# Attention scores and transposed weights of two heads in one two-bank PSUM tile, in a written order, the next unit's scores ahead of the softmax

## The chip, the cores and the metric

The kernel runs on one core of a Trainium2 chip. The time is the device time of one execution in microseconds; lower is better. Runs are compared with runs of the kernel before on the same chip.

## The reference, cut to what matters

One decoder layer on a sequence of 256 positions, all in float32: an input projection feeds three token mixers (a convolution module A, a spatial gating unit B and a sparse attention C), whose outputs are gated, added and projected, and a feed-forward part follows. The change concerns the attention C. It has 16 heads of width 64 in 4 groups and three branches that share the queries: compressed blocks, selected blocks and a window. At 256 positions the window and the selection both hold every earlier position, so these two branches are plain causal attention, each with its own keys and values:

```python
def masked_softmax(s, mask):
    s = jnp.where(mask, s.astype(jnp.float32), NEG)
    m = jnp.max(s, axis=-1, keepdims=True)
    e = jnp.where(mask, jnp.exp(s - m), 0.0)
    return e / jnp.maximum(jnp.sum(e, axis=-1, keepdims=True), 1e-30)
...
        s = jnp.einsum("bqghd,bkgd->bghqk", qb, kw)
        p = masked_softmax(s, wmask)
        o_win = jnp.einsum("bghqk,bkgd->bqghd", p.astype(vw.dtype), vw)
        gb = lax.dynamic_slice_in_dim(gates, start, NSA_Q_BLOCK, axis=1)
        return gb[..., 0:1] * o_cmp + gb[..., 1:2] * o_slc + gb[..., 2:3] * o_win
```

## The kernel before

The weights stream through: a piece of 128x1024 is fetched by SyncE, split by ScalarE (line 118, `whi`) and VectorE (line 119, `wlo`) into a high and a low half, and multiplied on TensorE in three products (lines 167 to 169, or 147 and 154). Four split pieces can stand ready; a piece feeds twelve matmuls of 512 columns in the stage of this case.

This stage is `branch(bi, ...)`, run for B, A and C in turn. For each of four column blocks it computes the merge gate (`pg`, from `hT`) and the output projection (`py`, from `Bt`, `At` or `Ct`). Small work of the mixers is written as generators in the queue `bg`; after each group of projection matmuls, `pump` takes steps from the first generator until their estimated times use up a budget. `until("C")` empties the queue up to the mark C before the third projection reads `Ct`. The order thus traced is a priority: a planner then places instructions on each engine, by its own estimates of when their inputs and buffers are ready, earlier ones first. `issue_after(ins)` forces an order on one engine.

The attention runs in the stages of B and A. `attn(qt, gg)` is traced for two query tiles of 128 positions and two head groups, and does two branches (`br`) in it: eight units (qt, gg, br), here numbered 0 to 7 in that order. A unit has four pairs of heads, j = 0..3, r = 0 and 1. Head r of a pair lies in partitions 64r to 64r+63 of `qf` and `kk`, so its score matmul (line 680) uses half of TensorE's rows; its value matmul (line 712) writes half of the columns, partitions 64r onward of `O`. There are 128 keys (qt = 0) or 256 (qt = 1). A unit's steps are: the scores into `ps`, per head r a tile of its own; VectorE adds the mask, takes the maximum and writes `e` (line 685); ScalarE takes the exponential and the sum (line 691) and scales by gate over sum (line 700); TensorE transposes the weights into `pp`, per r and key block (line 706); ScalarE copies them out (line 707); TensorE multiplies with the values into `O` (line 712). `O` starts with the compressed branch (line 664), takes both branches of a (qt, gg) and goes to `Ct`.

PSUM has eight banks: four for the tiles "acc" of the projections and four of the tag "bg", from which `O`, the score tiles, the weight tiles and the small tiles of the other generators (transposes of the input, layer norm sums, spatial gating, compression, merge) are drawn. The weights `e` and their transposes `pt` lie in SBUF tiles of the tag "s8", of which four exist and the keys and queries hold two. "s16" has three larger ones: `At`, `Bt`, `Ct` at this time, later `mh` and `ml`, the operands of the merge, traced ahead of the third branch.

Of the kernel before, what the change touches and what calls it, by code (L numbers as in the profile page):

```python
# [47 lines left out]
def block(ctx: ExitStack, tc: tile.TileContext, x, fp, cst, rows, sgw, w1, w2, wf_a, wt_bv, wf_bu, wf_c,  # L48
# [5 lines left out]
    P0 = ctx.enter_context(tc.tile_pool(name="p0", bufs=1))  # L54
    PS = ctx.enter_context(tc.tile_pool(name="ps", bufs=4, space=PSUM))

    def row(i0, n):
# [124 lines left out]

    marks = set()
    T1 = {}
# [85 lines left out]
    def enter(k):  # L270

        pt = PS.tile([128, T], F32, tag="bg", name=f"pth{k}")
# [50 lines left out]
    for cb in range(2):  # L323
# [26 lines left out]
        if cb == 0:  # L350
            r0 = norm1(ss, "x", 2)
            V.tensor_scalar(rh, r0, 0.5, None, op0=ALU.mult)
            rbp = PS.tile([128, T], F32, tag="bg", name="rbp")
# [51 lines left out]
    def lna_gen():  # L405
        def total(acc, nm):
            ps = PS.tile([128, T], F32, tag="bg", name="lnp" + nm)
            PE.matmul(ps, lhsT=ones, rhs=acc, start=True, stop=True)
            return ps
# [57 lines left out]
    def sg_gen(gi):  # L467
        ps = PS.tile([128, 2, 128], F32, tag="bg", name=f"psg{gi}")
# [61 lines left out]
    def cmp_gen(kv):  # L530
        bk = bk_box[kv]
        zp = PS.tile([128, 2, 256], F32, tag="bg", name=f"zp{kv}")
        for q in range(4):
# [10 lines left out]
        for a in range(2):  # L544
            S.activation(zs[a], zp[:, a], AF.Copy)
        hp = PS.tile([128, 2, 64], F32, tag="bg", name=f"hp{kv}")
        for h in range(2):
# [10 lines left out]
        if kv == 0:  # L558
            ps = PS.tile([128, 64], F32, tag="bg", name="kcp")
            for h in range(2):  # L560
# [4 lines left out]
        else:  # L565
# [6 lines left out]
            for gg in range(2):  # L572
                ps = PS.tile([128, 128], F32, tag="bg", name=f"vcp{gg}")
                for h in range(2):
# [46 lines left out]
    def cmp_attn(qt):  # L621
        ps = PS.tile([128, 2, 4, 2, 16], F32, tag="bg", name=f"sc{qt}")
        for gg in range(2):
# [25 lines left out]
        yield 1300  # L649
        pp = PS.tile([128, 2, 128], F32, tag="bg", name=f"pcp{qt}")  # L650
        for gg in range(2):
# [6 lines left out]

    def attn(qt, gg):


        O = PS.tile([128, 4, 128], F32, tag="bg", name=f"O{qt}{gg}")
        for j in range(4):
            PE.matmul(O[:, j], lhsT=vbd[:, gg, j], rhs=pct[qt][:, gg], start=(j == 0), stop=False,
                      skip_group_check=True)
        nk = (qt + 1) * 128
        mk = cs[:, K_MK + 256 - nk:K_MK + 256]
        hpb = 512 // nk
        half = [slice(0, 64), slice(64, 128)]
        for br in range(2):  # L670
            nm = f"{qt}{gg}{br}"
            ep = [s8([128, 2, 4, 256], F32, f"ep{nm}{r}") for r in range(2)]
            e = [t[:, 0] for t in ep]
            pt = [t[:, 1].rearrange("p a b -> p (a b)").rearrange("p (k c) -> p k c", k=2) for t in ep]
            m = P1.tile([128, 2, 8], F32, tag="am", bufs=2, name="am" + nm)
            for b in range(4 // hpb):
                ps = [PS.tile([128, hpb, nk], F32, tag="bg", name=f"s{nm}{b}{r}") for r in range(2)]
                for jj in range(hpb):
                    for r in range(2):
                        PE.matmul(ps[r][:, jj], lhsT=qf[half[r], gg * 4 + b * hpb + jj, qt * 128:qt * 128 + 128],  # L680
                                  rhs=kk[half[r], gg, br, 0:nk], start=True, stop=True)
                for jj in range(hpb):
                    j = b * hpb + jj
                    for r in range(2):
                        V.tensor_tensor_reduce(e[r][:, j, 0:nk], ps[r][:, jj], mk, 1.0, -3e38, ALU.add, ALU.max,
                                               m[:, r, j:j + 1])
                        yield nk * 1.05 + 130
            V.tensor_scalar(m[:, :, 0:4], m[:, :, 0:4], -1.0, None, op0=ALU.mult)
            for j in range(4):
                for r in range(2):  # L690
# [7 lines left out]
            for j in range(4):  # L698
                for r in range(2):
                    S.activation(e[r][:, j, 0:nk], e[r][:, j, 0:nk], AF.Copy, scale=m[:, r, 4 + j:5 + j])  # L700
                    yield 30
            for kb in range(qt + 1):
# [12 lines left out]
            yield 200  # L715
        Ct = Ct_box["t"]
        ch = Ct[:, gg * 4:gg * 4 + 4, 0, qt * 128:qt * 128 + 128]
        cl = Ct[:, gg * 4:gg * 4 + 4, 1, qt * 128:qt * 128 + 128]
        S.activation(ch, O, AF.Copy)
        V.tensor_sub(cl, O, ch.bitcast(F32))  # L720
        yield 650

# [14 lines left out]
    mac = s16(P0, [128, 2, D], F32, "mac")  # L737
    mh = ml = None

    def branch(bi, act_of):  # L740

        for cb in range(4):
# [43 lines left out]
    def mix_gen(cb):  # L786

        for k in range(4 * cb, 4 * cb + 4):
            pt = PS.tile([128, T], F32, tag="bg", name=f"pm{k}")
            for t in range(2):  # L790
                PE.transpose(pt[:, t * 128:t * 128 + 128], mac[:, t, k * 128:k * 128 + 128], ident)
            S.activation(mh[:, k], pt, AF.Copy, scale=0.5)
            V.scalar_tensor_tensor(ml[:, k], pt, 0.5, mh[:, k].bitcast(F32), op0=ALU.mult, op1=ALU.subtract)
            yield 500
# [3 lines left out]
    until("A")  # L798
    mh = s16(P1, [128, KT, T], R, "mh")
    ml = s16(P1, [128, KT, T], R, "ml")  # L800
    branch(2, lambda: Ct_box["t"])


# [37 lines left out]
    def enter2(t, k):  # L841

        pt = PS.tile([128, 128], F32, tag="bg", name=f"ptf{t}{k}")
        ts = slice(t * 128, t * 128 + 128)
# [91 lines left out]
    for run in lumps(pu2[2], hs, h2):  # L936
        in_line(run)
    rbp2 = PS.tile([128, T], F32, tag="bg", name="rbp2")
    with tc.issue_after(pe_last[0]):
# [194 lines left out]
```

## Time and profile before

| | us |
|---|---|
| median of 3 runs | 1621.16 |
| lowest and highest | 1620.5 and 1622.27 |
| the profiled execution | 1621.49 |
| its span in the profile | 1619.8 |
| TensorE busy with matmuls in it | 1599.5 (99%) |
| VectorE, ScalarE busy | 1125.6 (69%), 855.8 (53%) |

The span reaches from the first to the last instruction of the profiled execution. Busy times are sums over an engine's instructions without overlaps. In the views below a matmul's duration goes to its modelled end, and matmuls overlap, so what one costs in the line is read from the start of one to the start of the next. The tiles are given as written by the program without numbers: `s` scores, `pp` transposed weights, `O` values, `pg` and `py` projections.

### The profile page before, as it was taken

To read this page: it belongs to the slowest core of one execution; us is meant where nothing else is said; L and a number is where in the kernel's file an instruction comes from. 1 tells how busy PE (TensorE), PEld (TensorE's weight loads), DVE (VectorE), ACT (ScalarE), POOL (GpSimd) and SP (SyncE) were. 2 spreads that over 40 slices of the span, in tenths; PEclk is the share of its full clock that TensorE was granted. 3 is DMA by queue.
4 is the path that set the end of the run, shared out by engine and by line. 5 is a ranking of instruction groups with operands and counts; after the bars stand their busy time and mean duration, and the time that the engine had idled before them with its cause. 6 is when DMAs were issued, how large, how long until landed. Compare 5 with 4: busy or idle time off the path is not lost.

```text
span 1619.8 us, 22288 instructions
## 1 busy us (share of the span) xinstructions
PE 1599.5 (99%) x8293; PEld 1352.5 (84%) x8293; DVE 1125.6 (69%) x1914; ACT 855.8 (53%) x1378; POOL 16.1 (1%) x45
## 2 busy tenths in 40 slices
PE   9999998999999999999999999999999999999997
PEld 6888887888887767788888888888888888888886
DVE  6799999887655554455566877777777777444444
ACT  6554444475466655644455655555555555344342
POOL 0000020000000000000000000000000000000000
PEclk9999999999999999999999999999999999999999
DMA  8655556557644444555772655555555556666663
GB/s 296 226 197 182 186 157 200 184 181 244 204 144 155 159 130 139 186 185 191 239 249 83 195 190 189 187 192 192 185 189 193 190 184 201 212 193 194 192 192 115
DMA packets 85437, 303.74 MB, mean 188 GB/s; under 512 B 9808, under 2 KB 10192, under 8 KB 84688
## 3 DMA queue, kind: packets, MB, share of 16 engines
q1 hardware_dynamic: 84096, 298.04, 56.5%
q0 software_dynamic: 944, 4.19, 0.7%
q8 instruction: 65, 1.06, 0.3%
q14 instruction: 44, 0.36, 0.1%
q10 hardware_dynamic: 288, 0.08, 0.0%
HBM read 299.13 MB, written 2.10 MB: 186 GB/s over the span
## 4 chain that ended last, share of the span: by engine, by line
PE 96%; DVE 2%; DMA 1%; issue 0%; ACT 0%; SPq 0%; DVEq 0%; ACTq 0%
PE ps L147 28%; PE ps L154 15%; PE po L168 7%; PE po L169 7%; PE po L167 7%; PE pg L167 5%; PE pg L168 5%; PE pg L169 5%; PE py L167 3%; PE py L169 3%; PE py L168 3%; PE s L680 1%; PE pv L167 1%; PE O L712 1%; PE pv L168 1%; PE pv L169 1%
## 5 line engine op out<-in xcount | busy, mean ns | idle before, releaser
L119 DVE TENSOR_TENSOR wlo<-wraw,whi 128x1024 fp32r<-128x1024 f32 (+1 forms) x533 | 642.8, 1208 | 294.6 <-ACT whi L118 287.5
L118 ACT ACTIVATE whi<-wraw 128x1024 fp32r<-128x1024 f32 (+1 forms) x533 | 554.9, 1044 | 382.2 <-PE po L169 135.7
L147 PE MATMUL ps<-h2T,whi 128*128 128x512 f32 x1360 | 324.6, 391 | 0.0
L147 PEld LDWEIGHTS ps<-h2T,whi 128*128 128x128 f32 x1360 | 250.0, 188 | 48.3
L154 PEld LDWEIGHTS ps<-h2T,wlo 128*128 128x128 f32 x1360 | 174.4, 191 | 6.6
L154 PE MATMUL ps<-h2T,wlo 128*128 128x256 f32 x1360 | 176.7, 283 | 0.0
L147 PE MATMUL ps<-hT,whi 128*128 128x512 f32 x640 | 158.1, 394 | 3.1 <-ACT gsg L607 3.1
L169 PE MATMUL pg<-whi,hT 128*128 128x512 f32 x384 | 151.0, 393 | 0.0
L168 PE MATMUL pg<-wlo,hT 128*128 128x512 f32 x384 | 151.0, 393 | 0.0
L167 PE MATMUL pg<-whi,hT 128*128 128x512 f32 x384 | 148.9, 394 | 0.0
L190 ACT ACTIVATE t<-ps 128x256 f32<-128x256 f32 x125 | 47.5, 382 | 174.3 <-PE ps L147 174.3
L147 PEld LDWEIGHTS ps<-hT,whi 128*128 128x128 f32 x640 | 117.3, 190 | 25.3 <-ACT gsg L607 3.3
L167 PE MATMUL po<-whi,gh 128*128 128x512 f32 x336 | 130.7, 389 | 0.0
L168 PE MATMUL po<-wlo,gh 128*128 128x512 f32 x336 | 130.7, 389 | 0.0
L169 PE MATMUL po<-whi,gl 128*128 128x512 f32 x336 | 130.7, 389 | 0.0
L191 DVE TENSOR_TENSOR t<-ps,t 128x256 f32<-128x256 f32 x125 | 52.8, 423 | 91.6 <-ACT t L190 91.5
L401 DVE SCALAR_TENSOR_TENSOR cv<-hb,fps,cv 128x256 f32<-128x256 f32 x240 | 105.3, 479 | 0.8 <-ACT cv L397 0.7
L154 PEld LDWEIGHTS ps<-hT,wlo 128*128 128x128 f32 x640 | 84.4, 191 | 4.4
L154 PE MATMUL ps<-hT,wlo 128*128 128x256 f32 x640 | 86.1, 283 | 0.0
L169 PEld LDWEIGHTS pg<-whi,hT 128*128 128x128 f32 x384 | 72.1, 188 | 16.1 <-issue 1.5
L168 PEld LDWEIGHTS pg<-wlo,hT 128*128 128x128 f32 x384 | 72.1, 188 | 16.0 <-issue 1.3
L167 PEld LDWEIGHTS pg<-whi,hT 128*128 128x128 f32 x384 | 71.9, 188 | 15.6 <-issue 1.0
(297 smaller groups left out, 1923.0 us busy)
## 6 DMA issues: line engine op xcount, KB each, us to landing
wraw<-in_wf_up_dram SPq DMA_DIRECT2D x176, 512.0 KB, 4.2
wraw<-in_wt_g_dram SPq DMA_DIRECT2D x96, 512.0 KB, 3.7
wraw<-in_wt_dn_dram SPq DMA_DIRECT2D x88, 512.0 KB, 3.6
wraw<-in_wt_p_dram SPq DMA_DIRECT2D x48, 512.0 KB, 3.7
wraw<-in_wf_a_dram SPq DMA_DIRECT2D x32, 512.0 KB, 3.9
wraw<-in_wt_o_dram SPq DMA_DIRECT2D x32, 512.0 KB, 4.5
wraw<-in_wt_bv_dram SPq DMA_DIRECT2D x16, 512.0 KB, 6.3
wraw<-in_wf_bu_dram SPq DMA_DIRECT2D x16, 512.0 KB, 4.3
```

The costliest lines, as they stand in the source:

```text
L118: S.activation(hi[:, :n], raw[:, :n], AF.Copy)
L119: V.tensor_sub(lo[:, :n], raw[:, :n], hi[:, :n].bitcast(F32))
L147: ins = PE.matmul(ps[:, :, ts], lhsT=ws[k // 8][0][:, c:c + 128], rhs=mov[:, k, :, ts], start=(k == 0 and not t), stop=(k == n - 1), skip_ ...
L154: ins = PE.matmul(ps[:, 1, ts], lhsT=ws[k // 8][1][:, c:c + 128], rhs=mov[:, k, 0, ts], start=False, stop=False, skip_group_check=True).ins
L167: PE.matmul(ps, lhsT=xh, rhs=hi, start=first, stop=False)
L168: PE.matmul(ps, lhsT=xh, rhs=lo, start=False, stop=False)
L169: return PE.matmul(ps, lhsT=xl, rhs=hi, start=False, stop=last).ins
L190: S.activation(t1, ps[:, 1], AF.Copy)
L191: V.tensor_add(t1 if rb is not None else dst, ps[:, 0], t1)
L401: V.scalar_tensor_tensor(ca[:, j], hb[:, j, k:k + T], w(j, k), ca[:, j], op0=ALU.mult, op1=ALU.add)
L680: PE.matmul(ps[r][:, jj], lhsT=qf[half[r], gg * 4 + b * hpb + jj, qt * 128:qt * 128 + 128], rhs=kk[half[r], gg, br, 0:nk], start=True, sto ...
L712: PE.matmul(O[half[r]].rearrange("p j t -> p (j t)"), lhsT=vsw[:, kb, v0:v0 + 64], rhs=pt[r][:, kb], start=False, stop=((br, kb, r) == (1, ...
```

## The change

PSUM: the four single banks move into a pool of their own, which can be closed and reopened. For the attention it holds two single banks (`bank`, used by `O`) and one tile of two banks (`two_banks`); before and behind the attention it holds four singles again. `attn` becomes eight `Unit`s with three generators: `scores`, `weights` and `values`. The scores of both heads go to one two-bank tile, one bank for each r, and so do the transposed weights of a key block. The score matmuls and the value matmuls are chained by `in_turns`, r = 1 and r = 0 alternating, the values from the last key block to the first; the two copies out of a weight tile are chained too. The scores of unit n + 1 are traced before the softmax of unit n. The units of the second branch have `e` and `pt` in a tile `ep` of the tag "s16"; the compressed branch's matmuls come behind the first transposes; `mh` and `ml` are allocated behind `until("C")`. Elsewhere `PS.tile(..., tag="bg")` becomes `bank(...)`.

```diff
+    PB = {}
+    def banks(single, double):
+        if PB:
+            PB["ctx"].close()
+        PB["ctx"] = ctx.enter_context(ExitStack())
+        PB["pool"] = PB["ctx"].enter_context(tc.tile_pool(name=f"pb{single}{len(marks)}", bufs=single, space=PSUM))
+        PB["double"] = double
+    def bank(shape, name):
+        return PB["pool"].tile(shape, F32, tag="bg", name=name)
+    def two_banks(shape, name):
+        return PB["pool"].tile(shape, F32, tag="bg2", bufs=PB["double"], name=name)
...
+    banks(4, 0)
...
+    def in_turns(work):
+        last = None
+        for out, lhsT, rhs, start, stop in work:
+            with ExitStack() as order:
+                if last is not None:
+                    order.enter_context(tc.issue_after(last))
+                last = PE.matmul(out, lhsT=lhsT, rhs=rhs, start=start, stop=stop, skip_group_check=True).ins
...
+            ep = [Ct_box["ep"][:, r] if br else s8([128, 2, 4, 256], F32, f"ep{self.nm}{r}") for r in range(2)]
...
             for b in range(4 // hpb):
-                ps = [PS.tile([128, hpb, nk], F32, tag="bg", name=f"s{nm}{b}{r}") for r in range(2)]
-                for jj in range(hpb):
-                    for r in range(2):
-                        PE.matmul(ps[r][:, jj], lhsT=qf[half[r], gg * 4 + b * hpb + jj, qt * 128:qt * 128 + 128],
-                                  rhs=kk[half[r], gg, br, 0:nk], start=True, stop=True)
+                ps = two_banks([128, 2, hpb, nk], f"s{self.nm}{b}")
+                in_turns([(ps[:, r, jj], qf[half[r], gg * 4 + b * hpb + jj, qt * 128:qt * 128 + 128],
+                           kk[half[r], gg, br, 0:nk], True, True) for jj in range(hpb) for r in (1, 0)])
...
             for kb in range(qt + 1):
-                pp = [PS.tile([128, 4, 128], F32, tag="bg", name=f"pp{nm}{kb}{r}") for r in range(2)]
+                pp = two_banks([128, 2, 4, 128], f"pp{self.nm}{kb}")
                 for r in range(2):
                     for j in range(4):
-                        PE.transpose(pp[r][:, j], e[r][:, j, kb * 128:kb * 128 + 128], ident)
-                    S.activation(pt[r][:, kb], pp[r].rearrange("p j t -> p (j t)"), AF.Copy)
+                        PE.transpose(pp[:, r, j], e[r][:, j, kb * 128:kb * 128 + 128], ident)
+                for r in range(2):
+                    with ExitStack() as order:
+                        if r:
+                            order.enter_context(tc.issue_after(a))
+                        a = S.activation(pt[r][:, kb], pp[:, r].rearrange("p j t -> p (j t)"), AF.Copy).ins
                 yield 200
-            for kb in range(qt + 1):
-                for r in range(2):
-                    v0 = br * 256 + (2 * gg + r) * 64
-                    PE.matmul(O[half[r]].rearrange("p j t -> p (j t)"), lhsT=vsw[:, kb, v0:v0 + 64],
-                              rhs=pt[r][:, kb], start=False, stop=((br, kb, r) == (1, qt, 1)),
+            if br == 0:
+                for j in range(4):
+                    PE.matmul(O[:, j], lhsT=vbd[:, gg, j], rhs=pct[qt][:, gg], start=(j == 0), stop=False,
                               skip_group_check=True)
+            in_turns([(O[half[r]].rearrange("p j t -> p (j t)"),
+                       vsw[:, kb, br * 256 + (2 * gg + r) * 64:br * 256 + (2 * gg + r) * 64 + 64], pt[r][:, kb],
+                       False, (br, kb, r) == (1, 0, 0)) for kb in range(qt, -1, -1) for r in (1, 0)])
...
+    def attn():
+        units = [Unit(qt, gg, br) for qt in range(2) for gg in range(2) for br in range(2)]
+        yield from units[0].scores()
+        for n, u in enumerate(units):
+            if n + 1 < len(units):
+                yield from units[n + 1].scores()
+            yield from u.weights()
+            if u.at[2] == 0:
+                O = bank([128, 4, 128], "O" + u.nm)
+            yield from u.values(O)
...
     def alloc_C():
         Ct_box["t"] = s16(P1, [128, 8, 2, T], R, "Ct")
+        Ct_box["ep"] = s16(P1, [128, 2, 2, 4, T], F32, "ep")
+        banks(2, 1)
         yield 0
+    def single():
+        banks(4, 0)
+        yield 0
     bg.append(alloc_C())
-    for qt in range(2):
-        for gg in range(2):
-            bg.append(attn(qt, gg))
+    bg.append(attn())
+    bg.append(single())
     bg.append(mark("C"))
...
                 if cb == 0 and q == 0:
                     until("BAC"[bi])
+                    if bi == 2:
+                        mix["h"] = s16(P1, [128, KT, T], R, "mh")
+                        mix["l"] = s16(P1, [128, KT, T], R, "ml")
```

## Rows read from the trace of the kernel before

**Rows 1.** The page: the span, and the tenths of its full clock that TensorE was granted in 40 equal slices of it.
```profile
span 1619.8 us, 22288 instructions
...
PEclk9999999999999999999999999999999999999999
```

**Rows 2.** Who waited for whom on TensorE over the whole span: waiting tile and line, what released it, microseconds in total, times, longest. There are eight such rows; the first and the last stand here.
```profile
PE ps L147 <- ACT gsg L607: 3.1, 1, 3.1
...
PE pvs L167 <- DVE t L191: 0.4, 1, 0.4
```

**Rows 3.** The stretch of the attention, 454.60 to 673.04 us. First row: busy time of TensorE's matmuls, its weight loads, VectorE, ScalarE and GpSimd, with their instructions in brackets, then the granted clock, the DMA share and GB/s. Rows behind it: the attention's groups of matmuls in the same stretch (line, operation, tiles, shapes, count; busy time, mean ns of one).
```profile
454.60:673.04 218.44, 218.44 (x1027) 165.35 (x1026) 111.56 (x260) 134.74 (x305) 0.57 (x1) 1.00 0.47 151
...
L680 PE MATMUL s<-kkv,qf 64*128 64x128 f32 (+1 forms) x128 | 21.3, 346 | 0.0
L712 PE MATMUL O<-ep,kkv 128*64 128x512 f32 x48 | 16.3, 613 | 0.0
L706 PE MATMUL pp<-idn,ep 128*128 128x128 f32 x96 | 15.8, 273 | 0.0
...
L664 PE MATMUL O<-pct,vbd 128*128 128x128 f32 x32 | 4.9, 278 | 0.0
...
L652 PE MATMUL pcp<-idn,ce 128*128 128x128 f32 x2 | 0.4, 270 | 0.0
```

**Rows 4.** TensorE in order of time around a score visit whose two heads run side by side: start, duration to the modelled end of the last, line, tiles, shapes, count.
```profile
541.88 0.39 PE L169 MATMUL py<-whi,At 128*128 128x512 f32 x1
...
543.24 0.39 PE L169 MATMUL py<-whi,At 128*128 128x512 f32 x1
543.55 1.14 PE L680 MATMUL s<-kkv,qf 64*128 64x256 f32 x8
544.62 0.50 PE L167 MATMUL py<-whi,At 128*128 128x512 f32 x1
...
546.57 0.39 PE L169 MATMUL py<-whi,At 128*128 128x512 f32 x1
```

**Rows 5.** The same view of the scores of unit 1 (467.9 to 478.3 us), whose heads run one after the other.
```profile
468.58 0.93 PE L680 MATMUL s<-kkv,qf 64*128 64x128 f32 x6
...
470.14 0.48 PE L680 MATMUL s<-kkv,qf 64*128 64x128 f32 x2
...
476.55 1.16 PE L680 MATMUL s<-kkv,qf 64*128 64x128 f32 x8
477.63 0.50 PE L168 MATMUL pg<-wlo,hT 128*128 128x512 f32 x1
```

**Rows 6.** The same view from 566 to 577 us: the values of unit 4 and the scores of unit 5.
```profile
566.85 1.93 PE L712 MATMUL O<-ep,kkv 128*64 128x512 f32 x6
568.72 1.13 PE L680 MATMUL s<-kkv,qf 64*128 64x256 f32 x8
...
571.82 1.07 PE L712 MATMUL O<-ep,kkv 128*64 128x512 f32 x2
...
575.93 1.13 PE L680 MATMUL s<-kkv,qf 64*128 64x256 f32 x4
576.99 0.50 PE L167 MATMUL pg<-whi,hT 128*128 128x512 f32 x1
```

**Rows 7.** The same view of values followed at once by the next scores, both with their heads side by side.
```profile
536.84 0.39 PE L169 MATMUL py<-whi,At 128*128 128x512 f32 x1
537.15 1.08 PE L712 MATMUL O<-ep,kkv 128*64 128x512 f32 x4
...
539.23 0.50 PE L167 MATMUL py<-whi,At 128*128 128x512 f32 x1
...
541.65 0.39 PE L168 MATMUL py<-wlo,At 128*128 128x512 f32 x1
```

**Rows 8.** The same view of the values of the last unit.
```profile
665.55 0.39 PE L168 MATMUL pg<-wlo,hT 128*128 128x512 f32 x1
665.79 0.60 PE L706 MATMUL pp<-idn,ep 128*128 128x128 f32 x4
666.32 1.93 PE L712 MATMUL O<-ep,kkv 128*64 128x512 f32 x6
...
669.67 0.39 PE L169 MATMUL pg<-whi,hT 128*128 128x512 f32 x1
```

**Rows 9.** The same view of six transposes of weights among other matmuls.
```profile
593.01 0.81 PE L706 MATMUL pp<-idn,ep 128*128 128x128 f32 x6
...
593.89 0.39 PE L169 MATMUL pg<-whi,hT 128*128 128x512 f32 x1
```

**Rows 10.** ScalarE and VectorE in the stretch 454.60 to 673.04 us, shapes kept apart: line, operation, tiles, shapes, count; busy time, mean ns; idle time before it and what ended most of it.
```profile
L118 ACT ACTIVATE whi<-wraw 128x1024 fp32r<-128x1024 f32 x60 | 62.9, 1055 | 52.5 <-PE pg L169 35.4 <-PE py L169 15.3 <-issue 1.3
...
L707 ACT ACTIVATE ep<-pp 128x512 f32<-128x512 f32 x24 | 13.0, 597 | 16.1 <-PE pp L706 16.1
...
L685 DVE CUSTOM_DVE_ANT_0 ep<-s,cs 128x256 f32<-128x256 f32 x32 | 12.2, 421 | 14.3 <-PE s L680 11.6 <-PE O L712 2.6
...
L685 DVE DVE_READ_ACCUMULATOR2_ANT am<- 128x1 f32 x64 | 5.3, 83 | 0.0
```

**Rows 11.** Two tiles: an instruction that reads the second branch's activations Bt, and one that reads the attention's result Ct, with ns min/median/max and the first and last start.
```profile
L169 PE MATMUL py<-whi,Bt x64: 387/389/397, 340.0 to 465.7; 128*128 128x512 f32 x64
...
L167 PE MATMUL py<-whi,Ct x64: 389/389/393, 669.9 to 782.1; 128*128 128x512 f32 x64
```

More of the change, by code (lines that the diff above doesn't have):

```diff
@@ L181, in mark @@
         yield 0
-    marks = set()
     T1 = {}
@@ L270, in enter @@
     def enter(k):
-        pt = PS.tile([128, T], F32, tag="bg", name=f"pth{k}")
+        pt = bank([128, T], f"pth{k}")
         for t in range(2):
@@ L352, in block @@
             V.tensor_scalar(rh, r0, 0.5, None, op0=ALU.mult)
-            rbp = PS.tile([128, T], F32, tag="bg", name="rbp")
+            rbp = bank([128, T], "rbp")
             for t in range(2):
@@ L406, in total @@
         def total(acc, nm):
-            ps = PS.tile([128, T], F32, tag="bg", name="lnp" + nm)
+            ps = bank([128, T], "lnp" + nm)
             PE.matmul(ps, lhsT=ones, rhs=acc, start=True, stop=True)
@@ L467, in sg_gen @@
     def sg_gen(gi):
-        ps = PS.tile([128, 2, 128], F32, tag="bg", name=f"psg{gi}")
+        ps = bank([128, 2, 128], f"psg{gi}")
         for t in range(2):
@@ L531, in cmp_gen @@
         bk = bk_box[kv]
-        zp = PS.tile([128, 2, 256], F32, tag="bg", name=f"zp{kv}")
+        zp = bank([128, 2, 256], f"zp{kv}")
         for q in range(4):
@@ L545, in cmp_gen @@
             S.activation(zs[a], zp[:, a], AF.Copy)
-        hp = PS.tile([128, 2, 64], F32, tag="bg", name=f"hp{kv}")
+        hp = bank([128, 2, 64], f"hp{kv}")
         for h in range(2):
@@ L558, in cmp_gen @@
         if kv == 0:
-            ps = PS.tile([128, 64], F32, tag="bg", name="kcp")
+            ps = bank([128, 64], "kcp")
             for h in range(2):
@@ L572, in cmp_gen @@
             for gg in range(2):
-                ps = PS.tile([128, 128], F32, tag="bg", name=f"vcp{gg}")
+                ps = bank([128, 128], f"vcp{gg}")
                 for h in range(2):
@@ L621, in cmp_attn @@
     def cmp_attn(qt):
-        ps = PS.tile([128, 2, 4, 2, 16], F32, tag="bg", name=f"sc{qt}")
+        ps = bank([128, 2, 4, 2, 16], f"sc{qt}")
         for gg in range(2):
@@ L649, in cmp_attn @@
         yield 1300
-        pp = PS.tile([128, 2, 128], F32, tag="bg", name=f"pcp{qt}")
+        pp = bank([128, 2, 128], f"pcp{qt}")
         for gg in range(2):
@@ L657, in block @@
     pct = {}
[L659 to L675, printed above, removed]
-            for b in range(4 // hpb):
-                ps = [PS.tile([128, hpb, nk], F32, tag="bg", name=f"s{nm}{b}{r}") for r in range(2)]
-                for jj in range(hpb):
-                    for r in range(2):
-                        PE.matmul(ps[r][:, jj], lhsT=qf[half[r], gg * 4 + b * hpb + jj, qt * 128:qt * 128 + 128],
-                                  rhs=kk[half[r], gg, br, 0:nk], start=True, stop=True)
@@ new lines, in in_turns, with __init__, scores @@
+    def in_turns(work):
[5 more added lines that the diff above has]
+                last = PE.matmul(out, lhsT=lhsT, rhs=rhs, start=start, stop=stop, skip_group_check=True).ins
+    half = [slice(0, 64), slice(64, 128)]
+    class Unit:
+        def __init__(self, qt, gg, br):
+            self.at = qt, gg, br
+            self.nm = f"{qt}{gg}{br}"
+        def scores(self):
+            qt, gg, br = self.at
+            nk = (qt + 1) * 128
+            mk = cs[:, K_MK + 256 - nk:K_MK + 256]
+            hpb = 512 // nk
+            ep = [Ct_box["ep"][:, r] if br else s8([128, 2, 4, 256], F32, f"ep{self.nm}{r}") for r in range(2)]
+            e = self.e = [t[:, 0] for t in ep]
+            self.pt = [t[:, 1].rearrange("p a b -> p (a b)").rearrange("p (k c) -> p k c", k=2) for t in ep]
+            m = self.m = P1.tile([128, 2, 8], F32, tag="am", bufs=2, name="am" + self.nm)
+            for b in range(4 // hpb):
+                ps = two_banks([128, 2, hpb, nk], f"s{self.nm}{b}")
+                in_turns([(ps[:, r, jj], qf[half[r], gg * 4 + b * hpb + jj, qt * 128:qt * 128 + 128],
+                           kk[half[r], gg, br, 0:nk], True, True) for jj in range(hpb) for r in (1, 0)])
@@ L684, in attn @@
                     for r in range(2):
-                        V.tensor_tensor_reduce(e[r][:, j, 0:nk], ps[r][:, jj], mk, 1.0, -3e38, ALU.add, ALU.max,
+                        V.tensor_tensor_reduce(e[r][:, j, 0:nk], ps[:, r, jj], mk, 1.0, -3e38, ALU.add, ALU.max,
                                                m[:, r, j:j + 1])
@@ L688, in attn, with weights @@
             V.tensor_scalar(m[:, :, 0:4], m[:, :, 0:4], -1.0, None, op0=ALU.mult)
+        def weights(self):
+            qt, gg, br = self.at
+            e, m, nk = self.e, self.m, (qt + 1) * 128
             for j in range(4):
@@ L701, in attn, with values @@
                     yield 30
+        def values(self, O):
+            qt, gg, br = self.at
+            e, pt = self.e, self.pt
             for kb in range(qt + 1):
-                pp = [PS.tile([128, 4, 128], F32, tag="bg", name=f"pp{nm}{kb}{r}") for r in range(2)]
+                pp = two_banks([128, 2, 4, 128], f"pp{self.nm}{kb}")
                 for r in range(2):
                     for j in range(4):
-                        PE.transpose(pp[r][:, j], e[r][:, j, kb * 128:kb * 128 + 128], ident)
-                    S.activation(pt[r][:, kb], pp[r].rearrange("p j t -> p (j t)"), AF.Copy)
@@ L715, in attn @@
             yield 200
[L716 to L721, printed above, removed]
+            if br == 0:
+                return
+            Ct = Ct_box["t"]
+            ch = Ct[:, gg * 4:gg * 4 + 4, 0, qt * 128:qt * 128 + 128]
+            cl = Ct[:, gg * 4:gg * 4 + 4, 1, qt * 128:qt * 128 + 128]
@@ new lines, in values @@
+            S.activation(ch, O, AF.Copy)
+            V.tensor_sub(cl, O, ch.bitcast(F32))
+            yield 650
+    def attn():
[8 more added lines that the diff above has]
+            yield from u.values(O)
@@ L737, in block @@
     mac = s16(P0, [128, 2, D], F32, "mac")
-    mh = ml = None
+    mix = {}
     def branch(bi, act_of):
@@ L788, in mix_gen @@
         for k in range(4 * cb, 4 * cb + 4):
-            pt = PS.tile([128, T], F32, tag="bg", name=f"pm{k}")
+            pt = bank([128, T], f"pm{k}")
             for t in range(2):
                 PE.transpose(pt[:, t * 128:t * 128 + 128], mac[:, t, k * 128:k * 128 + 128], ident)
-            S.activation(mh[:, k], pt, AF.Copy, scale=0.5)
-            V.scalar_tensor_tensor(ml[:, k], pt, 0.5, mh[:, k].bitcast(F32), op0=ALU.mult, op1=ALU.subtract)
+            S.activation(mix["h"][:, k], pt, AF.Copy, scale=0.5)
+            V.scalar_tensor_tensor(mix["l"][:, k], pt, 0.5, mix["h"][:, k].bitcast(F32), op0=ALU.mult,
+                                   op1=ALU.subtract)
             yield 500
@@ L841, in enter2 @@
     def enter2(t, k):
-        pt = PS.tile([128, 128], F32, tag="bg", name=f"ptf{t}{k}")
+        pt = bank([128, 128], f"ptf{t}{k}")
         ts = slice(t * 128, t * 128 + 128)
@@ L937, in block @@
         in_line(run)
-    rbp2 = PS.tile([128, T], F32, tag="bg", name="rbp2")
+    rbp2 = bank([128, T], "rbp2")
     with tc.issue_after(pe_last[0]):
```

4 lines of the change are left out of this document (2 added, 2 removed).

## The prediction, made before the change was built

> **What bounds the kernel now.** I read four views. The page comes first: the span is 1619.8 us and the granted clock is at full in all 40 slices [rows 1], so no stretch is slow because of the clock. The waits of TensorE come second: there are eight in all, the longest 3.1 us, and none is at a matmul of the attention (lines 664, 680, 706, 712) [rows 2]. The third view is the stretch that the change touches: from 454.60 to 673.04 us TensorE is busy for 218.44 of 218.44 us, while ScalarE is busy for 134.74 and VectorE for 111.56 [rows 3]. So TensorE sets the end here, it waits for nobody, and time can be gained only by making its own instructions take less of its line.
>
> The fourth view, TensorE in order of time, tells what they take. The gate and output projections run at a steady pitch: six steps from 541.88 to 543.24 us, 0.227 us each [rows 4]. Of the 1027 matmuls of the stretch 128 are scores, 48 values, 96 transposes, 32 compressed values and 2 compressed weights [rows 3], which leaves 721 at that pitch; one of these straddles the left edge, and at 0.2267 us the 720 others take 163.2 us. From 454.60 to the next projection after the last values (0.1 us past the window's end) are 218.5 us. **The attention now costs TensorE 218.5 - 163.2 = 55.3 us**, the price that the change can move.
>
> Part of it is paid twice. A head of a pair uses half of TensorE's rows (scores) or columns (values). Where the two heads alternate they run side by side: eight score matmuls of 256 columns take 1.07 us, 543.55 to 544.62 [rows 4]. Where they don't, four take 1.06 us, 575.93 to 576.99 [rows 6]. Unit 1 has its scores in three pieces, 468.58, 470.14 and 476.55 us, the last being eight in 1.08 us [rows 5]. The values show the same: 6 matmuls take 1.87 us and 2 more come 5 us later, at 571.82, in a visit of their own [rows 6], where 4 took 1.01 us as two steps [rows 7]. (The code issues 64 score matmuls and 24 value matmuls; the trace shows twice as many, each being run as two.)
>
> **The change part by part.** Each time TensorE turns from projections to scores or values and back I call a visit; its price is the time from the last undisturbed projection before to the first after, less 0.2267 us for each projection begun in it.
>
> (a) A score visit, heads side by side: 543.24 to 546.57 us is 3.33, less nine projections, 1.29 us [rows 4]. Eight serial matmuls of 128 columns take 1.08 us [rows 5], so eight side-by-side pairs of them, a whole unit of the first query tile, cost about the same, 1.30.
> (b) Values and next scores in one visit: 536.84 to 541.65 us is 4.81, less eleven projections, 2.32 us, with two value steps in it [rows 7].
> (c) A value step: 566.85 to 568.72 us holds four, 537.15 plus 1.01 us two, so 0.43 us each [rows 6, 7].
> (d) Four value steps alone: 665.55 to 669.67 us is 4.12, less seven projections, 2.53, less the four transposes in it, 0.44: 2.09 us [rows 8]. A transpose is (593.89 - 593.01 - 0.23)/6 = 0.109 us [rows 9].
>
> After the change a unit's scores lie in one tile of two banks, so both heads' banks come free at once, and the written order alternates them; the same for the values, whose order begins with the block whose weights arrive last, so all eight are ready when the first is. The next unit's scores and this unit's values both wait for the same event, the copy of the transposed weights out of the one two-bank tile, so I expect them next to each other. That gives: scores of units 0 and 1 alone, 2 x 1.30; values 0 to 3 each with the scores (or first half of them) of units 2 to 5, 4 x 2.32; values 4 and 5, with two more steps each, 2 x (2.32 + 0.86); second halves of the scores of units 4 to 7, 4 x 1.29; values 6 and 7 alone, 2 x 2.09. Sum 27.6 us. The 130 transposes and compressed matmuls stay, 130 x 0.109 = 14.2, and I add 1.0 for their edges (in rows 9 the edge is under 0.1). **After: 42.8 us, a gain of 12.5.** If values and scores do not meet, a pair of visits costs (2.09 - 0.86) + 1.29 = 2.52 in place of 2.32, six times: the gain is 11.3. I take 12.0.
>
> (e) The double tile has one copy, where four single banks served before. A score tile is held until VectorE has taken it out, four times 0.421 + 0.083 = 2.0 us for 256 columns; a weights tile until ScalarE has copied it twice, 1.2 us [rows 10]. I cost this at nothing, because projections fill TensorE meanwhile, as they did where unit 1's second half waited six microseconds for a bank [rows 5] without an idle TensorE. Without that cover it is the second rival below.
> (f) The second branch of each unit keeps its weights in a third large buffer, which is free when the projection's last read of Bt has begun, 465.7 us [rows 11]. Unit 0's scores can be out of the double tile by about 460 us (454.6, 1.3 for the scores, at most eight copies of 0.5), so unit 1's may wait on VectorE for some 6 us; queued behind them are the splits of the weights, which TensorE needs. Now unit 1's second half begins at 476.55 [rows 5], so this is no new delay for the attention. For the splits 6 us lie under the stock of four split pieces, twelve projections each, 4 x 2.7 = 10.9 us; uncovered they cost 6 us at most.
> (g) The scores of the next unit ahead of the softmax take their length out of the chain of units, and with it some waiting of VectorE (14.3 us) [rows 10]; TensorE did not wait for that chain, so alone it is worth nothing. It only must end in time: the first read of the result Ct is at 669.9 us [rows 11], and comes 12 us sooner.
> (h) The pools that are closed and reopened and the later allocation of the merge's buffers add no instruction; they lie where cmp_attn's tiles are already copied out and before the merge's first transposes. Nothing.
>
> The profiled execution took 1621.49 us, 0.3 above the median of the runs, 1621.16. 1621.49 - 12.0 = 1609.5; against the median 1609.2. The forecast is **1609.3 us**. A measurement of this kernel can tell about 0.2% (3.2 us) from no change.
>
> **The rivals.** First, *the heads alternate only in part*, because other ready matmuls get between them. For it speaks that now, with no such order, they are apart as often as together; against it that all are ready at once. Half the pairs of (a) and (c) lost would be about half of the gain: 1615.5.
>
> Second, on the other side, *TensorE stands before the two-bank tile*. If the order on TensorE puts a score or a transpose at a place where the tile is not yet free, everything behind it waits. The eight score tiles of the second query tile cost up to 2.0 us each, the four of the first up to 4.0 (eight copies), the twelve weights tiles 1.2: 16 + 16 + 14.3 = 46 us, so up to 1655; from 12 us on, half a microsecond per tile, the kernel is slower. Against it: banks were short before as well and no wait of TensorE shows [rows 2]. The Trainium skill, TensorEngine Tiling (Array Packing), section PSUM Bottleneck, says that tiling speeds up TensorE but not the emptying of PSUM, which may then be the bottleneck. By that rule the time would go this way; the trace shows the emptying (2.0 us) longer than the 1.07 us of matmuls, but a tile only every few microseconds.
>
> Third, *the gain is eaten by late splits*: ScalarE holds the splits (62.9 us, and 52.5 us in which it waits in front of them) beside the attention [rows 10], and the attention's work comes in a shorter time. With 8 to 12 us of stalls the time is 1618 to 1622, no change. Against it: ScalarE is busy for 134.74 of 218.44 us [rows 3].
>
> **How the numbers follow.** The forecast (gain 9 to 13.5) 0.66; the first rival, or a few microseconds of stalls, 0.19; the third 0.08; the second with a loss over 3.2 us 0.07. Faster by over 0.2% takes the first two cases, 0.85; same 0.08; slower 0.07. The range begins at 1607, a gain of 14 (all transitions cheaper than (a) to (d)), and ends at 1617, where the first rival lies with stalls of 1.5 us on top.
>
> **What would show it.** In TensorE's order of time: score visits as x16 (first query tile) or x8 in about 1.1 us, values as x4 in 1.0 or x8 in 1.9 us, none as x2 or x6; about 14 visits of scores or values; the stretch shorter by 12 us with the same 720 projections. Wrong would be: new waits of TensorE at lines of scores or transposes, or score groups of x4 in 1.06 us. If the gain is there in the stretch but not in the span, a later stretch has taken it.

## The result and the profile after

| | before | after |
|---|---|---|
| median of the runs, us | 1620.83 (4 runs) | 1608.41 (4 runs) |
| lowest and highest | 1620.06 to 1622.27 | 1607.68 to 1609.14 |
| ratio to before, 95% interval | | 0.9921 [0.9909, 0.9933] |
| the profiled execution; its span | 1621.49; 1619.8 | 1607.9; 1606.2 |

The change makes the kernel 12.4 us faster. The page after, with the rows that answer to [rows 1]:

```profile
span 1606.2 us, 22284 instructions
...
PE 1586.2 (99%) x8293; PEld 1346.7 (84%) x8293; DVE 1125.6 (70%) x1914; ACT 855.0 (53%) x1378; POOL 16.1 (1%) x45
...
PEclk9999999999999999999999999999999999999999
```

TensorE's waits over the whole span (waiting line, releaser, total us, times, longest; the first of seven rows), for [rows 2]; none of the seven is at the attention.

```profile
PE ps L165 <- ACT gsg L625: 3.9, 1, 3.9
```

The stretch of the attention with TensorE's groups in it (columns as in [rows 3]); scores and values now stand in one helper, line 685:

```profile
454.09:650.93 196.84, 196.84 (x991) 153.22 (x989) 106.84 (x257) 129.07 (x297) 0.57 (x1) 1.00 0.51 160
...
L685 PE MATMUL s<-kkv,qf 64*128 64x128 f32 (+1 forms) x128 | 13.7, 343 | 0.0
L743 PE MATMUL pp<-idn,ep 128*128 128x128 f32 x96 | 12.5, 273 | 0.0
L685 PE MATMUL O<-ep,kkv 128*64 128x512 f32 x48 | 12.1, 609 | 0.0
...
L752 PE MATMUL O<-pct,vbd 128*128 128x128 f32 x32 | 4.7, 284 | 0.0
L670 PE MATMUL pcp<-idn,ce 128*128 128x128 f32 x2 | 0.4, 270 | 0.0
```

The count is read as before. Of the 991 matmuls 306 are the attention's, so 685 projections, of which 684 begin in the stretch. From its start, 454.09 us, to the first projection behind the last values, 651.24 us, are 197.15 us; less 684 x 0.2267 = 155.1, **the attention costs TensorE 42.1 us, where it cost 55.3: 13.2 us less.** The spans differ by 13.6; the other 0.4 lies in the first 320 us, where the change only alters the pool of the small tiles, and executions of one kernel differ by more (1620.06 to 1622.27 us before).

TensorE in order of time (start, duration, line, tiles, shapes, count), for [rows 4 to 8]:

```profile
466.63 1.16 PE L685 MATMUL s<-kkv,qf 64*128 64x128 f32 x16
467.73 0.50 PE L187 MATMUL pg<-whi,hT 128*128 128x512 f32 x1
...
516.84 1.08 PE L685 MATMUL O<-ep,kkv 128*64 128x512 f32 x4
517.85 1.13 PE L685 MATMUL s<-kkv,qf 64*128 64x256 f32 x8
518.91 0.50 PE L185 MATMUL pg<-whi,hT 128*128 128x512 f32 x1
...
525.05 1.13 PE L685 MATMUL s<-kkv,qf 64*128 64x256 f32 x8
526.12 0.50 PE L187 MATMUL pg<-whi,hT 128*128 128x512 f32 x1
...
570.98 1.94 PE L685 MATMUL O<-ep,kkv 128*64 128x512 f32 x8
572.85 1.13 PE L685 MATMUL s<-kkv,qf 64*128 64x256 f32 x8
573.91 0.50 PE L187 MATMUL pg<-whi,hT 128*128 128x512 f32 x1
...
634.67 1.94 PE L685 MATMUL O<-ep,kkv 128*64 128x512 f32 x8
636.54 1.09 PE L743 MATMUL pp<-idn,ep 128*128 128x128 f32 x8
...
649.37 1.94 PE L685 MATMUL O<-ep,kkv 128*64 128x512 f32 x8
651.24 0.50 PE L185 MATMUL pg<-whi,hT 128*128 128x512 f32 x1
```

Every score visit holds all sixteen matmuls of a unit (or eight, half a unit of the second query tile) in 1.07 to 1.10 us; values come as four in 1.01 or eight in 1.87 us, and the scores of the unit after next begin the instant they end (516.84 and 517.85, 570.98 and 572.85). There are 14 visits, where the kernel before had 24, a visit counted here as a run of scores and values that no other matmul breaks; by the prediction's own words, from projections and back to them, there were 20 before and are 14 after. The x2 and x6 groups of before [rows 5, 6] are gone. The attention ends with the last part of the result, at 652.0 us (an instruction of the tile Ct, with its count, ns min/median/max, first and last start), for [rows 11]:

```profile
L764 DVE TENSOR_TENSOR Ct<-O,Ct x4: 686/692/692, 503.3 to 652.0; 128x512 fp32r<-128x512 f32 x4
```

### The profile page after: what moved, and what is told of

It is laid out like the page before. It is cut to its first block, busy times and chain, and to the rows that moved or that the text cites. A ratio compares the mean times of both kernels' runs of the same rounds, so it can differ in the third digit from the quotient of the medians.

```text
span 1606.2 us, 22284 instructions
## 1 busy us (share of the span) xinstructions
PE 1586.2 (99%) x8293; PEld 1346.7 (84%) x8293; DVE 1125.6 (70%) x1914; ACT 855.0 (53%) x1378; POOL 16.1 (1%) x45
## 4 chain that ended last, share of the span: by engine, by line
PE 96%; DVE 2%; issue 0%; DMA 0%; ACT 0%; SPq 0%; DVEq 0%; ACTq 0%
PE ps L165 28%; PE ps L172 15%; PE po L186 7%; PE po L187 7%; PE po L185 7%; PE pg L185 5%; PE pg L187 5%; PE pg L186 5%; PE py L186 3%; PE py L187 3%; PE py L185 3%; DVE cv L419 1%; PE pv L185 1%; PE pv L186 1%; PE pv L187 1%; PE s L685 1%
```

## The experiments

All were timed against the kernel before, in five rounds; an edit is one to the changed kernel where nothing else is said. What they should tell apart: is the gain TensorE's own time in its visits (heads side by side, fewer turns), or the shorter chain of units; and which part of the change brings it, the tile, the order or the scores ahead?

**Heads apart in each chain.**

```diff
-                           kk[half[r], gg, br, 0:nk], True, True) for jj in range(hpb) for r in (1, 0)])
+                           kk[half[r], gg, br, 0:nk], True, True) for r in (1, 0) for jj in range(hpb)])
...
-                       False, (br, kb, r) == (1, 0, 0)) for kb in range(qt, -1, -1) for r in (1, 0)])
+                       False, (br, kb, r) == (1, 0, 0)) for r in (1, 0) for kb in range(qt, -1, -1)])
```

> The changed kernel, but in each chain all matmuls of head r = 1 come before those of r = 0, so that two heads meet only where one ends and the other begins. Nothing else moves: TensorE has the same visits at the same places. Theory (the gain is heads side by side plus fewer visits): a unit's 16 score matmuls of 128 columns take 15 steps of 0.112 us in place of 8, eight of 256 take 7 steps of 0.216 in place of 4, the values 3 or 7 steps of 0.43 in place of 2 or 4. That is 4 x 0.78 + 8 x 0.65 + 4 x 0.43 + 4 x 1.29 = 15.2 us more: about 1623.6, a little slower than the kernel before. Rival (the gain comes from the shorter chain of units, the scores being ahead of the softmax): 1608 to 1610.

Measured: 1610.97 us, ratio 0.9940 [0.9927, 0.9954]. My theory was wrong by 12.6 us in its number. TensorE in order of time:

```profile
460.00 1.71 PE L685 MATMUL s<-kkv,qf 64*128 64x128 f32 x16
461.64 1.16 PE L752 MATMUL O<-pct,vbd 128*128 128x128 f32 x8
...
528.00 1.14 PE L685 MATMUL s<-kkv,qf 64*128 64x256 f32 x8
529.07 0.50 PE L187 MATMUL pg<-whi,hT 128*128 128x512 f32 x1
...
573.95 1.94 PE L685 MATMUL O<-ep,kkv 128*64 128x512 f32 x8
575.82 1.14 PE L685 MATMUL s<-kkv,qf 64*128 64x256 f32 x8
```

The sixteen matmuls of a unit of 128 keys take 1.64 us in place of 1.10; four times that difference is 2.2 us, nearly all of the 2.6 that was lost by the medians. The eight of a half unit still take 1.07 us and the eight of the values 1.87 us, though in the program two matmuls of one head stand before two of the other. The trace has two records for each matmul; those at 528.00 us start in pairs, 0.013 us apart in a pair and 0.32, then 0.216 us from pair to pair, while four of one half alone start 0.32, then 0.216 us apart (575.93 us in [rows 6]). So TensorE brought the heads together itself: it started matmuls that use the other half of its rows or columns ahead of some that stand before them. Over two matmuls it did so, over four only in part. This run thus did not set the heads apart as it was meant to, and by itself it does not decide between the theory and the rival.

**Groups of two.**

```diff
-                           kk[half[r], gg, br, 0:nk], True, True) for jj in range(hpb) for r in (1, 0)])
+                           kk[half[r], gg, br, 0:nk], True, True) for j2 in range(0, hpb, 2) for r in (1, 0) for jj in (j2, j2 + 1)])
...
-                       False, (br, kb, r) == (1, 0, 0)) for kb in range(qt, -1, -1) for r in (1, 0)])
+                       False, (br, kb, r) == (1, 0, 0)) for r in (1, 0) for kb in range(qt, -1, -1)])
```

> The changed kernel with the score chains in groups of two matmuls for each head (r = 1 twice, r = 0 twice, and so on) and the values with both of r = 1 before both of r = 0. In the run with all of r = 1 ahead, tiles of two head pairs still ran side by side and only the tiles of four did not. Theory (TensorE starts a matmul of the other half of its rows though up to two matmuls stand before it): everything runs side by side and the time is that of the changed kernel, 1607.5 to 1609.5. Rival (what counts there was something else in the longer tiles): about 2.6 us more.

Measured: 1607.89 us, ratio 0.9919 [0.9905, 0.9932], the changed kernel's time. The unit of 128 keys:

```profile
460.03 1.26 PE L685 MATMUL s<-kkv,qf 64*128 64x128 f32 x16
461.22 1.16 PE L752 MATMUL O<-pct,vbd 128*128 128x128 f32 x8
```

It takes 1.19 us, 0.09 over the strict alternation, and far from 1.64. So writing the heads strictly in turns, and not two by two, is worth next to nothing. The chain itself adds nothing to the changed kernel: without it (the helper without its `issue_after`) the program has TensorE's instructions in the same order, one by one. What the heads need is to be ready in one visit.

**The written order alone, on the kernel before.**

```diff
-                for jj in range(hpb):
-                    for r in range(2):
-                        PE.matmul(ps[r][:, jj], lhsT=qf[half[r], gg * 4 + b * hpb + jj, qt * 128:qt * 128 + 128],
-                                  rhs=kk[half[r], gg, br, 0:nk], start=True, stop=True)
+                in_turns([(ps[r][:, jj], qf[half[r], gg * 4 + b * hpb + jj, qt * 128:qt * 128 + 128],
+                           kk[half[r], gg, br, 0:nk], True, True) for jj in range(hpb) for r in (1, 0)])
...
```

(and the values' chain of the change in place of their loop.)

> The kernel before with the written order alone: scores and values chained with r = 1 and r = 0 in turn, values from the last key block, on the single banks as before. Theory: all values and most scores come side by side, but a chain whose second bank is not free leaves its first matmul in a visit of its own; some 22 visits in place of 14 in the changed kernel, 8 x 0.45 = 3.6 us, and single score matmuls of 0.2 to 0.4 us, 2.4 us: 1613 to 1616, about half of the gain. Rival (the order is all that counts): 1608 to 1610. Rival (the two-bank tile is all that counts): 1619 to 1622.

Measured: 1614.94 us, ratio 0.9962 [0.9950, 0.9975]: about half of the gain, as the theory had it. Unit 4's scores in order of time:

```profile
538.85 0.70 PE L665 MATMUL s<-kkv,qf 64*128 64x256 f32 x2
...
540.92 1.13 PE L665 MATMUL s<-kkv,qf 64*128 64x256 f32 x6
...
546.73 0.70 PE L665 MATMUL s<-kkv,qf 64*128 64x256 f32 x2
...
548.25 1.13 PE L665 MATMUL s<-kkv,qf 64*128 64x256 f32 x6
```

A first score matmul, run as two, goes off alone at 538.85 and again at 546.73 us; the chain holds the rest back, which then come as x6. That the plan has no second bank for the other head at that point fits this, but the trace doesn't name the bank. Each such start is a turn of TensorE for one matmul.

**The two-bank tile alone, on the kernel before.**

```diff
-                ps = [PS.tile([128, hpb, nk], F32, tag="bg", name=f"s{nm}{b}{r}") for r in range(2)]
+                ps2 = two_banks([128, 2, hpb, nk], f"s{nm}{b}")
+                ps = [ps2[:, r] for r in range(2)]
...
-                pp = [PS.tile([128, 4, 128], F32, tag="bg", name=f"pp{nm}{kb}{r}") for r in range(2)]
+                pp2 = two_banks([128, 2, 4, 128], f"pp{nm}{kb}")
+                pp = [pp2[:, r] for r in range(2)]
```

(with the pools of the change.)

> The kernel before with the two-bank tile alone: scores and transposed weights of both heads in it, two single banks beside it during the attention, no chains, no scores ahead, transposes and copies traced head by head as before. Theory: all scores come side by side, but one head's transposes and copy follow the other's and the values become ready one head at a time, so they come singly: a visit of 1.23 us more for each unit of the first query tile and 2.83 us more for each of the second than in the changed kernel, 4 x 1.23 + 4 x 2.83 = 16.2 us: 1622 to 1626, slower than the kernel before though all scores are side by side. Rival (the tile is what counts): 1608 to 1612.

Measured: 1637.07 us, ratio 1.0104 [1.0090, 1.0118], slower than before by 16.7 us, where I had expected 2 to 5. The turns are as expected: the values come head by head, each two behind four transposes, in unit 0 for instance at 479.05 and 484.36 us.

```profile
478.52 0.60 PE L725 MATMUL pp<-idn,ep 128*128 128x128 f32 x4
479.05 1.07 PE L731 MATMUL O<-ep,kkv 128*64 128x512 f32 x2
...
484.36 1.07 PE L731 MATMUL O<-ep,kkv 128*64 128x512 f32 x2
```

What I had left out is the length of the chain. The first read of the result is at 648.6 us, and the last part of the result is written at 724.2 (two instructions of the tile Ct, columns as for the changed kernel):

```profile
L184 PE MATMUL py<-whi,Ct x64: 388/389/504, 648.6 to 797.2; 128*128 128x512 f32 x64
...
L739 DVE TENSOR_TENSOR Ct<-O,Ct x4: 684/690/692, 515.3 to 724.2; 128x512 fp32r<-128x512 f32 x4
```

By then the projections that need nothing more of it are used up, and TensorE waits for ScalarE's scaled weights (wait, total us, times, longest):

```profile
PE pp L725 <- ACT ep L718: 6.5, 5, 5.3
```

Busy time by stretch (columns as in [rows 3]):

```profile
695.00:720.00 25.00, 18.05 (x69) 10.73 (x69) 8.60 (x27) 12.81 (x33) 0.57 (x1) 0.81 0.33 114
707.00:710.00 3.00, 0.00 (x0) 0.00 (x0) 1.06 (x4) 3.00 (x14) 0.00 (x0) 1.00 0.86 303
713.00:716.00 3.00, 1.67 (x6) 0.91 (x6) 0.00 (x0) 2.24 (x6) 0.00 (x0) 0.50 0.00 0
```

From 695 to 720 us TensorE is idle for 7 of 25 us, and after the longest wait its granted clock is 0.50, the 1.2 GHz level. Two records of values, 1.07 us at 479.05, take longer there:

```profile
716.50 1.97 PE L731 MATMUL O<-ep,kkv 128*64 128x512 f32 x2
```

So the tile alone costs twice: in turns, and in a chain that ends too late. The values' order is not the whole reason: in the run "The values as before" below they are traced as here, with the rest of the change beside them (transposes of both heads together, scores ahead), and the time is 1614.78 us. Which of these keeps the chain short was not taken apart.

**No scores ahead of the softmax.**

```diff
-        yield from units[0].scores()
         for n, u in enumerate(units):
-            if n + 1 < len(units):
-                yield from units[n + 1].scores()
+            yield from u.scores()
             yield from u.weights()
```

> The changed kernel, but a unit's scores are traced behind the values of the unit before, not ahead of its softmax. Theory (TensorE's own time in the visits is the gain; the chain of units is not on the path): values and next scores still meet, so the price of the attention stays within 1.5 us of the changed kernel's 42, the attention ends some 15 to 20 us later, and the time is 1607 to 1610. Rival (scores ahead of the softmax make the gain): most of the 12.4 us is lost, 1616 to 1621. A third outcome: the attention ends after the first use of Ct at 657.5 us and TensorE waits, over 1611.

Measured: 1609.51 us, ratio 0.9932 [0.9919, 0.9944], which can't be told from the changed kernel's. Values and the next scores still share a visit:

```profile
551.86 1.08 PE L685 MATMUL O<-ep,kkv 128*64 128x512 f32 x4
552.86 1.13 PE L685 MATMUL s<-kkv,qf 64*128 64x256 f32 x8
```

The attention ends at 698.1 us, 46 us later than with the scores ahead (652.0) and not the 15 to 20 expected, and TensorE hardly waits: only the second query tile's part of the result is that late. The price of the attention, counted as before, is 2.5 us above the changed kernel's and so outside the 1.5 expected (in an execution of 1611.0 us, the slowest of the five): 1.0 us are short waits, the longest 0.5, and the transposes come in 35 groups, where the changed kernel has 12.

```profile
L764 DVE TENSOR_TENSOR Ct<-O,Ct x4: 681/692/692, 507.4 to 698.1; 128x512 fp32r<-128x512 f32 x4
```

**The values as before.** The chain of the values is replaced by the loop of the kernel before (first key block first, r = 0 first).

> The changed kernel with the value matmuls as before: first key block first, r = 0 ahead of r = 1, no chain. Theory: for the first query tile nothing changes. For the second the first key block's values are ready before the second block's transposes, and come among them in a visit of their own, the heads apart: per unit two steps of 0.43 us more and some 0.75 us for the turns, 4 x 1.6 = 6.5 us: 1613 to 1616. Rival (the order of the values is of no account once heads share a tile): 1607.5 to 1609.5.

Measured: 1614.78 us, ratio 0.9962 [0.9949, 0.9974]. A unit of the second query tile:

```profile
559.04 1.07 PE L757 MATMUL O<-ep,kkv 128*64 128x512 f32 x2
560.05 1.09 PE L743 MATMUL pp<-idn,ep 128*128 128x128 f32 x8
561.07 1.07 PE L757 MATMUL O<-ep,kkv 128*64 128x512 f32 x2
```

The first key block's values stand around the second block's transposes, one head on each side; that visit takes 3.0 us for work that takes 1.8 with the values side by side (1.01 for the values, 0.79 for eight transposes). So of the written orders it is the values' that counts, because it holds them back until all are ready.

**More visits, no more matmuls.**

```diff
-            hpb = 512 // nk
+            hpb = 2
...
-                ps = two_banks([128, 2, hpb, nk], f"s{self.nm}{b}")
+                ps = two_banks([128, 2, 512 // nk, nk], f"s{self.nm}{b}")
```

> The changed kernel with the scores of the first query tile in two tiles of two head pairs each, as in the second: four more score visits, no more matmuls. Theory (a lone visit costs 0.45 us beside its matmuls): 4 x 0.45 = 1.8 us more, 1609.5 to 1611, and in the trace 14 visits become 18. Rival (turning to half the rows and back costs nothing that counts, only pairs do): no more than 0.3 us.

Measured: 1610.04 us, ratio 0.9929 [0.9917, 0.9942], 1.6 us over the changed kernel by the medians and 1.3 by the ratios; the intervals overlap, so the price is better read in the trace, at one such half visit:

```profile
473.42 0.39 PE L187 MATMUL pg<-whi,hT 128*128 128x512 f32 x1
473.73 0.72 PE L685 MATMUL s<-kkv,qf 64*128 64x128 f32 x8
474.38 0.50 PE L185 MATMUL pg<-whi,hT 128*128 128x512 f32 x1
...
475.41 0.40 PE L186 MATMUL pg<-wlo,hT 128*128 128x512 f32 x1
```

From 473.42 to 475.41 us are 1.99 us; less five projections, 0.86 (0.87 with the last of the turn). Two halves are 1.73, the whole visit in the changed kernel 1.32 by the same reading: a turn costs 0.42 us.

**The two-bank tile emptied twice.**

```diff
-                        V.tensor_tensor_reduce(e[r][:, j, 0:nk], ps[:, r, jj], mk, 1.0, -3e38, ALU.add, ALU.max,
-                                               m[:, r, j:j + 1])
+                        for _ in range(2):
+                            V.tensor_tensor_reduce(e[r][:, j, 0:nk], ps[:, r, jj], mk, 1.0, -3e38, ALU.add, ALU.max,
+                                                   m[:, r, j:j + 1])
```

> The changed kernel with each copy of scores out of the two-bank tile done twice (the same result written again): 64 more copies, 26.6 us of VectorE, and a score tile held 2 us (256 keys) or 3 us (128 keys) longer. Theory (TensorE fills the time with projections): the attention ends later, but before its result is used, and the time stays at 1607.5 to 1609.5. Rival (the emptying of the one two-bank tile sets the pace): 8 x 2.0 + 4 x 3.0 = 28 us more.

Measured: 1607.57 us, ratio 0.9914 [0.9900, 0.9928], no slower. VectorE does the copies twice (64 of 256 columns, 25.3 us, where the changed kernel has 32), and the attention ends at 685.4 us. VectorE's group in the stretch, and the tile Ct's row:

```profile
L715 DVE CUSTOM_DVE_ANT_0 ep<-s,cs 128x256 f32<-128x256 f32 x64 | 25.3, 421 | 5.1 <-PE s L685 4.2
```

```profile
L765 DVE TENSOR_TENSOR Ct<-O,Ct x4: 691/692/692, 512.9 to 685.4; 128x512 fp32r<-128x512 f32 x4
```

TensorE has no wait at the attention here either. The attention does end 33 us later (685.4 against 652.0), more than the 28 us that the copies hold the tile longer, so the doubled copies do lengthen the chain of the units by about what the rival counted, through the tile or through VectorE's own time. TensorE has projections to run meanwhile, and the time does not follow.

## Why the prediction was right, point by point

**The bound.** TensorE was without a gap before and is after, and the time fell by what its own instructions take less: 13.2 us in the stretch against 12.4 in the medians.

**The sum.** It said 42.8 us after, 27.6 for the visits; the trace shows 42.1. The visits are the ones listed in it, in their order. The small differences: unit 6's values stand next to transposes, which saves a turn, and the transposes' edges were priced at 1.0 us, which was too much. The forecast, 1609.3 us, was 0.9 too slow, because I took 12.0 between 11.3 and 12.5: values and next scores do meet, every time.

**Where the gain lies.** The visits fell from 24 to 14 (by the count of unbroken runs above); ten turns at 0.42 us are 4.2 us, a third of the 13.2. The rest should be the heads side by side, and the trace lets it be counted. A record is called alone here when no other of its kind starts within 0.05 us of it:

| | scores alone, of 128 | values alone, of 48 |
|---|---|---|
| the kernel before | 64 | 16 |
| the written order alone | 36 | 0 |
| the two-bank tile alone | 0 | 48 |
| changed kernel, values as before | 0 | 20 |
| changed kernel, heads apart | 40 | 0 |
| changed kernel, groups of two | 8 | 0 |
| the changed kernel | 0 | 0 |

Two records alone cost a step more than a pair. Of the 64 scores alone before, 32 have 128 columns and 32 have 256: 16 x 0.112 + 16 x 0.216 + 8 x 0.43 (values) = 8.7 us, an estimate from the steps of [rows 4 to 7]. With the turns, those from transposes taken to cost as much as those from projections, that is 12.9 of the 13.2 us. The table also tells the parts of the change apart: the tile brings all scores together, the written order all values.

**One step was right for another reason.** The prediction put the side-by-side running down to the written alternation. The two runs with the order loosened show that TensorE does it over a distance of two matmuls. Its own example shows the same: at 543.55 us [rows 4] the program of the kernel before has both matmuls of r = 0 ahead of both of r = 1. That the scores ran apart before because their banks came free at different times is borne out by the table: with the two-bank tile in place of single banks, and nothing else changed, none is alone; with the order on single banks 36 are. The order alone gave half of the gain and the tile alone a loss. In the changed kernel the transposes are also traced together ahead of both copies, and the values are held until all are ready; the second is worth 6.4 us (the run with the values as before), the first was not run by itself.

**The scores ahead** were put at nothing. The run without them is 1.1 us slower by the medians, which the intervals can't tell from nothing, and 2.5 us dearer in its profiled execution. The condition named with it, that the attention must end in time, is a real one, but it lies much later than I had it: at 698.1 us TensorE had 1.0 us of short waits, at 724.2 it stood idle for 7 us and then ran at half its clock.

**The rivals.** The first, partial alternation, is what the order alone gives (1614.9, forecast for the rival 1615.5); in the changed kernel no record is alone. The second, TensorE standing before the two-bank tile, did not happen, not even with the emptying doubled. The section PSUM Bottleneck of the Trainium skill's TensorEngine Tiling (Array Packing) says that the copying out of PSUM may become the bottleneck once tiling has sped TensorE up. The time here, 1607.57 us with the copies of scores doubled, does not bear that out. For these copies the traces show why: they take 2.0 us a tile [rows 10], and the tiles come 7.2 us apart (517.85 and 525.05 us above). The third, late splits, shows in no wait of TensorE; VectorE's wait for scores fell from 11.6 us [rows 10] to 3.1:

```profile
L714 DVE CUSTOM_DVE_ANT_0 ep<-s,cs 128x256 f32<-128x256 f32 x32 | 11.7, 420 | 3.1 <-PE s L685 3.1
```

**The delay of unit 1** at the buffer freed by Bt was no cost either: its scores ran at 466.63 us, 10 us earlier than the last of them before [rows 5].

## What to carry to other kernels

Where small matmuls that use half of TensorE interrupt a stream that fills it, price each interruption: its steps with both halves in use, plus a fixed turn (0.42 us here). Then make whatever the two halves need, PSUM banks above all, come free in one event, and hold a group back until all of it is ready; between matmuls that are ready together an order finer than two by two adds next to nothing (at most 0.09 us a visit here). Measure the parts of such a change apart, since here one part alone loses 16.7 us, and the whole gains 12.4.

## What the runs showed of the hardware that was not expected

TensorE ran matmuls of the two halves of its rows, or of its columns, side by side though two of one half stood before two of the other (eight records of values in 1.87 us, eight of scores in 1.07), with four before four only in part (1.64 us in place of 1.10). After an idle stretch of 5.3 us in the run with the tile alone the granted clock stood at 0.50 from 713 to 716 us, before the attention's last matmuls were through, and two records of values took 1.97 us there in place of 1.07: that idle wait in an otherwise full TensorE cost more than its length.
